# High parts of the weight blocks by a casting DMA from GpSimd in place of a ScalarE cast

## The chip, the cores and the metric

One core of a Trainium2 chip. The metric is the device time of one execution in microseconds, the median of three runs. Engines are called as in the profile: PE (TensorE, with PEld for its weight loads), DVE (VectorE), ACT (ScalarE), POOL (GpSimd), SP (SyncE); SPq is SP's queue of DMA issues.

## The reference

One layer of a streaming encoder on 512 prompt frames and 64 frames of a running stream, model width 1024. All in fp32:

```
proj = rmsnorm(x) @ w_in                      # 1024 x 7880, split by columns
hm   = mlstm(conv(proj_x), proj_v, gates) * sigmoid(proj_o)
ha   = attention(latents of proj_cq, proj_ckv, proj_kr)
p_m  = (hm * silu(proj_z)) @ w_pm
p_a  = (ha * silu(proj_za)) @ w_pa
y    = x + (sigmoid(g_m) * p_m + sigmoid(g_a) * p_a) @ w_out
```

The mLSTM has 4 heads of width 256, the attention 8 heads of 128 + 64. Updated caches and states are outputs too.

## The kernel before

Activations lie transposed, features on the partitions and all T = 576 frames on the free axis. To keep fp32 precision with products in fp32r, every operand is held as a high part (the value rounded to fp32r) and a low part (the rest), and each product is made of three: high x high, high x low and low x high.

A weight block is fetched by `wload` (L103): SP issues the load of `raw` (two buffers), `split_of` (L99) has ACT round it into `whi` and DVE subtract that from `raw` into `wlo` (two buffers each). There are 88 such blocks. 64 of them are blocks of 1024 x 128 weights (56 of w_in, 8 of w_pm, by `fblock`, L146); the others are 8 of w_pa (256 x 512), 4 of w_ukv (256 x 512), 4 of w_uq (384 x 384), 4 of wq_m and wk_m together (two sources of 256 x 256), and 4 of w_out (512 x 256). All are 512 KB but w_uq (576 KB). The blocks of w_ukv and w_uq have their high and low parts in a pool of their own (`cw`), which is opened after the first stage; `wts`, which holds the others, is open from the beginning. The blocks of the first stage (`load_a`, `load_b`) and the second halves of w_out (L843) use `split_of` without `wload`.

A block of `fblock` is multiplied by `gemm_f` (L116) in two halves of 288 frames, each in a PSUM bank of its own (`MM`, L57; one pair of banks, so a half must be emptied before the same half of the next block begins). A half takes whi x high (8 products), whi x low (8), wlo x high (8). The banks are emptied by ACT for the blocks of g_m, g_a, the conv input, the output gate and the values, by DVE also for the two SiLU gates (L520, L685), the added parts of p_a (L597) and p_m (L829).

The order of the work: a first stage (norm, latent projections, mLSTM gates) after START, then attention after PLAN, in which letters stand for tiles of k and q (K), blocks of gates (G, Z), heads (H) and p_a (P); then the mLSTM heads with their blocks between them, p_m, and w_out. The instructions of each engine run in the order of a queue; the framework's scheduler sets that order when the program is built, from its planned times, and inserts the waits. `rsqrt_of` (L74), which every norm uses, is a `pow` on POOL: for k and q tiles (L492, L449: tiles `r`), for the mLSTM chunks (L790: `sc`). POOL issues no DMA.

Of the kernel before, what the change touches and what calls it, by code (L numbers as in the profile page):

```python
# [6 lines left out]
F32 = mybir.dt.float32  # L7
# [3 lines left out]
ALU = mybir.AluOpType  # L11
AX = mybir.AxisListType

P = 128
# [24 lines left out]
def layer(ctx: ExitStack, tc, A, O):  # L39
    nc = tc.nc  # L40
    act, dve, pool, pe, sp = nc.scalar, nc.vector, nc.gpsimd, nc.tensor, nc.sync
# [57 lines left out]
    def split_of(hi, lo, src, eng=None):  # L99
        act.copy(hi, src)  # L100
        (eng or dve).tensor_tensor(lo, src, hi.bitcast(F32), op=ALU.subtract)  # L101

    def wload(srcs, nk, n, wp=None, unit=1024):  # L103
        wp = wp or wts
        shp = lambda t: t[:, 0:nk * n].rearrange("p (k c) -> p k c", k=nk)
        raw = shp(wts.tile([P, 6 * QH], F32, tag="raw", name="raw", bufs=2))
        o = 0
        for s in srcs:
            sp.dma_start(raw[:, o:o + s.shape[0] // P], s.rearrange("(k p) c -> p k c", p=P))
            o += s.shape[0] // P  # L110
        hi = shp(wp.tile([P, unit], F32R, tag="whi", name="whi", bufs=2))
        lo = shp(wp.tile([P, unit], F32R, tag="wlo", name="wlo", bufs=2))
        split_of(hi, lo, raw)
        return hi, lo

    def gemm_f(ps, w, x, nk, c0=0, k0=0):  # L116
# [29 lines left out]
    def fblock(wd, col, x):  # L146
        w = wload([wd[:, col:col + P]], KB, P)
        ps = MM()
        gemm_f(ps, w, x, KB)
        return ps  # L150
# [274 lines left out]
    with ExitStack() as es:  # L425
# [139 lines left out]
        def kq(p):  # L565
            qT = [aq.tile([P, TP], F32, tag="qT", name="qT", bufs=4) for _ in range(2)]
            qrT = aq.tile([P, 2, TP], F32R, tag="qrT", name="qrT", bufs=2)
            for hh in range(2):
                pool.memset(qT[hh][:, T:TP], 0.0)
            pool.memset(qrT.bitcast(F32)[:, :, T:TP], 0.0)  # L570
            kT = [ak.tile([P, TK], F32, tag="kT", name="kT", bufs=4) for _ in range(2)]
            v = ak.tile([P, 6, 2, VD], F32, tag="v", name="v", bufs=2)
            pool.memset(v[DEC:P, 5], 0.0)
            wk = wload([A["w_ukv"][:, 512 * p:512 * (p + 1)]], 2, 512, cw, 6 * QH)
            wq = wload([A["w_uq"][:, 2 * QH * p:2 * QH * (p + 1)]], 3, 2 * QH, cw, 6 * QH)
            run = []
            for g in [k_tile(wk, n, kT, v) for n in range(6)] + [q_tile(wq, n, qT, qrT) for n in range(5)]:
                next(g)
                run.append(g)
                if len(run) > 2:  # L580
                    next(run.pop(0))
            for g in run:
                next(g)
            return qT, qrT, kT, v
# [41 lines left out]
    with ExitStack() as es:  # L626
# [209 lines left out]
        for nb in range(D // NB):  # L836
            cs = slice(nb * NB, (nb + 1) * NB)
            w = [wload([A["w_out"][0:512, cs]], 4, NB)]
            raw = lp.tile([P, 4, NB], F32, tag="gate", name="wraw", bufs=2)
            sp.dma_start(raw, A["w_out"][512:D, cs].rearrange("(k p) c -> p k c", p=P))  # L840
            hi = lp.tile([P, 4, NB], F32R, tag=("qf", "kf")[nb % 2], name="whi2", bufs=1)
            lo = lp.tile([P, 4, NB], F32R, tag=("tm", "ulo")[nb % 2], name="wlo2", bufs=1)
# [69 lines left out]
```

## Time and profile before

| | before |
|---|---|
| median of 3 runs (lowest, highest) | 808.32 us (808.09, 808.92) |
| the profiled execution's own time | 810.22 us |
| its span, first to last instruction | 808.4 us |
| mean granted clock of PE | 0.998 |
| busy PE / DVE / ACT / POOL | 98 / 60 / 45 / 18% |
| data moved by DMA | 72.8 MB |

The profiled execution is one of its own, so sums of its rows are compared with its 810.22 us. Busy time of PE is of pipelined products, whose ends are modelled.

### The profile page before, as it was taken

To read this page: it belongs to the slowest core of one execution; us is meant where nothing else is said; L and a number is where in the kernel's file an instruction comes from. 1 tells how busy PE (TensorE), PEld (TensorE's weight loads), DVE (VectorE), ACT (ScalarE), POOL (GpSimd) and SP (SyncE) were. 2 spreads that over 40 slices of the span, in tenths; PEclk is the share of its full clock that TensorE was granted. 3 is DMA by queue.
4 is the path that set the end of the run, shared out by engine and by line. 5 is a ranking of instruction groups with operands and counts; after the bars stand their busy time and mean duration, and the time that the engine had idled before them with its cause. 6 is when DMAs were issued, how large, how long until landed. Compare 5 with 4: busy or idle time off the path is not lost.

```text
span 808.4 us, 14939 instructions
## 1 busy us (share of the span) xinstructions
PE 791.6 (98%) x5727; PEld 762.3 (94%) x5727; DVE 481.0 (60%) x1240; ACT 362.2 (45%) x991; POOL 148.2 (18%) x286
## 2 busy tenths in 40 slices
PE   7899999999999999989999999999999999999998
PEld 6898998899899898879999999999999999999997
DVE  5567667765686668545535872775587356555421
ACT  5546646663555554414334545444554434322100
POOL 2354331510251134001002111110211111000000
PEclk9999999999999999999999999999999999999999
DMA  8531331023123021314323242333344332533332
GB/s 268 142 110 60 81 108 27 1 54 106 42 53 123 27 67 31 104 35 129 80 79 105 65 119 69 89 85 99 93 129 111 91 87 75 163 111 107 101 102 72
DMA packets 101743, 72.81 MB, mean 90 GB/s; under 512 B 5742, under 2 KB 95848, under 8 KB 101672
## 3 DMA queue, kind: packets, MB, share of 16 engines
q1 hardware_dynamic: 101672, 71.86, 30.8%
q8 instruction: 45, 0.74, 0.4%
q14 instruction: 26, 0.21, 0.1%
HBM read 64.24 MB, written 7.61 MB: 89 GB/s over the span
## 4 chain that ended last, share of the span: by engine, by line
PE 91%; DVE 4%; DMA 3%; ACT 1%; issue 1%; SPq 0%; POOL 0%; ACTq 0%; POOLq 0%
PE mm L122 58%; PE sk L139 9%; PE sa L858 3%; PE sk L858 3%; PE sa L733 2%; PE sa L557 2%; PE sk L733 2%; PE sk L132 2%; PE sa L528 2%; PE sk L750 1%; PE sa L546 1%; PE sa L132 1%; PE sa L530 1%; DMA part<-in_w_in 1%; PE sk L498 1%; DMA E<-gscr 1%
## 5 line engine op out<-in xcount | busy, mean ns | idle before, releaser
L101 DVE TENSOR_TENSOR wlo<-raw,whi 128x1024 fp32r<-128x1024 f32 (+1 forms) x88 | 108.8, 1237 | 95.2 <-ACT whi L100 89.1
L100 ACT CAST whi<-raw 128x1024 fp32r<-128x1024 f32 (+1 forms) x88 | 92.7, 1054 | 136.6 <-PE mm L122 94.1
L122 PE MATMUL mm<-hhi,whi 128*128 128x288 f32 x896 | 146.1, 299 | 1.0 <-ACT hhi L100 1.0
L122 PE MATMUL mm<-hhi,wlo 128*128 128x288 f32 x896 | 146.7, 298 | 0.0
L122 PE MATMUL mm<-hlo,whi 128*128 128x288 f32 x896 | 145.7, 298 | 0.0
L122 PEld LDWEIGHTS mm<-hhi,whi 128*128 128x128 f32 x896 | 126.3, 188 | 2.5 <-ACT hhi L100 1.3
L122 PEld LDWEIGHTS mm<-hlo,whi 128*128 128x128 f32 x896 | 127.1, 188 | 0.9 <-issue 0.5
L122 PEld LDWEIGHTS mm<-hhi,wlo 128*128 128x128 f32 x896 | 127.1, 188 | 0.5
L75 POOL TENSOR_TENSOR r<-r,mhalf 128x2 f32<-128x2 f32 (+3 forms) x44 | 37.0, 841 | 126.1 <-DVE r L491 85.7
L122 PE MATMUL mm<-ha,whi 128*128 128x288 f32 x256 | 50.3, 314 | 2.0 <-ACT ha L100 1.2
L122 PEld LDWEIGHTS mm<-ha,whi 128*128 128x128 f32 x256 | 39.0, 194 | 5.4 <-DVE part L597 2.2
L122 PE MATMUL mm<-ha,wlo 128*128 128x288 f32 x128 | 27.8, 300 | 0.0
L75 POOL TENSOR_TENSOR sc<-sc,mhalf 128x1 f32<-128x1 f32 x20 | 12.1, 605 | 84.9 <-DVE sc L789 84.9
L597 DVE TENSOR_TENSOR part<-part,mm 128x288 f32<-128x288 f32 x48 | 21.2, 449 | 8.6 <-PE mm L122 8.4
L664 POOL MEMSET vf<- 128x64 f32 x8 | 1.2, 152 | 131.8 <-PE sk L673 72.2
L101 POOL TENSOR_TENSOR qi<-qi,qi 128x256 fp32r<-128x256 f32 x16 | 11.8, 737 | 71.6 <-ACT qi L100 71.6
L510 ACT ACTIVATE P<-sa,sc 128x128 f32<-128x128 f32 (+3 forms) x32 | 16.9, 527 | 16.7 <-DVE sc L509 16.5
L528 PE MATMUL sa<-kT,qT 128*128 128x128 f32 (+3 forms) x64 | 22.7, 435 | 0.5 <-ACT qT L470 0.5
L470 ACT ACTIVATE qT<-sk,gqn_c 128x128 f32<-128x128 f32 (+1 forms) x40 | 12.1, 352 | 21.6 <-PE sk L468 21.6
L733 PE MATMUL sk<-va,kw 128*128 128x258 f32 x120 | 21.5, 284 | 0.1
L829 DVE SCALAR_TENSOR_TENSOR mt<-tgm,mm 128x288 f32<-128x288 f32 x16 | 7.3, 454 | 23.9 <-PE mm L122 23.9
L122 PEld LDWEIGHTS mm<-ha,wlo 128*128 128x128 f32 x128 | 21.0, 192 | 0.0
(356 smaller groups left out, 1660.1 us busy)
## 6 DMA issues: line engine op xcount, KB each, us to landing
raw<-in_w_in SPq DMA_DIRECT2D x56, 512.0 KB, 3.9
raw<-in_w_pa SPq DMA_DIRECT2D x8, 512.0 KB
raw<-in_w_pm SPq DMA_DIRECT2D x8, 512.0 KB
raw<-in_w_uq SPq DMA_DIRECT2D x4, 576.0 KB, 4.0
gmscr<-tg SPq DMA_DIRECT2D x8, 288.0 KB
tgm<-gmscr SPq DMA_DIRECT2D x8, 288.0 KB, 2.7
xt<-in_x_prompt SPq DMA_DIRECT2D x4, 512.0 KB, 6.7
raw<-in_w_ukv SPq DMA_DIRECT2D x4, 512.0 KB, 3.4
```

Source lines behind the costliest of these rows:

```text
L75: pool.tensor_tensor(dst, ms, mhalf[0:n, 0:dst.shape[-1]], op=ALU.pow)
L100: act.copy(hi, src)
L101: (eng or dve).tensor_tensor(lo, src, hi.bitcast(F32), op=ALU.subtract)
L122: pe.matmul(ps[j], a[:, k0 + k, c0:c0 + P], b[:, k, sl], start=(n == 0), stop=(n == len(trip) - 1))
L132: pe.matmul(out, x[:, k, t0:t0 + P], a, start=(i == 0), stop=(i == len(trip) - 1))
L139: pe.matmul(out, b[:, k, t0:t0 + L], a[:, k, c0:c0 + n], start=(i == 0), stop=(i == len(trip) - 1))
L510: act.activation(pt[0:L, 0:n], ps, AF.Exp, bias=sc[0:L, 0:1], accum_out=sc[0:L, 1:2])
L528: pe.matmul(ps[:, 0:n], qT[hh][:, q0:q0 + P], kT[hh][:, 0:n], start=True, stop=False)
L557: pe.matmul(of[:, j * P:SEQ], v[:, j, hh], pT[:, off[j]:off[j] + (4 - j) * P], start=(j == 0), stop=(j == 3))
L597: dve.tensor_tensor(part[:, f, sl], part[:, f, sl], ps[j], op=ALU.add)
L733: pe.matmul(out, x, y, start=(first and i == 0), stop=(last and i == 2))
L858: pe.matmul(ps[0:L, 0:NB], x[:, 4 * u + k, t0:t0 + L], w[u][i][:, k], start=(q == 0), stop=(q == len(trip) - 1))
```

## The change

The high part is no longer made by ACT from `raw` but fetched a second time from memory by a DMA that POOL issues and that casts fp32 to fp32r on its way; DVE subtracts it from `raw` as before. A block of two sources takes two such DMAs. The scratch memory for descriptors of DMAs issued by the program is made larger.

```diff
@@ wload @@
         hi = shp(wp.tile([P, unit], F32R, tag="whi", name="whi", bufs=2))
         lo = shp(wp.tile([P, unit], F32R, tag="wlo", name="wlo", bufs=2))
-        split_of(hi, lo, raw)
+        o = 0
+        for s in srcs:
+            pool.dma_start(hi[:, o:o + s.shape[0] // P], s.rearrange("(k p) c -> p k c", p=P))
+            o += s.shape[0] // P
+        dve.tensor_tensor(lo, raw, hi.bitcast(F32), op=ALU.subtract)
         return hi, lo
@@ kernel @@
-    nc = _bacc.Bacc("TRN2", target_bir_lowering=False, num_devices=1, dynamic_dma_scratch_size=1024)
+    nc = _bacc.Bacc("TRN2", target_bir_lowering=False, num_devices=1, dynamic_dma_scratch_size=4096)
```

## Rows read from the trace of the kernel before

**Rows 1.** The page: busy time of each engine, and the granted clock by slices.
```profile
span 808.4 us, 14939 instructions
PE 791.6 (98%) x5727; PEld 762.3 (94%) x5727; DVE 481.0 (60%) x1240; ACT 362.2 (45%) x991; POOL 148.2 (18%) x286
PEclk9999999999999999999999999999999999999999
```

**Rows 2.** Table by stage: length, busy us of each engine, clock, DMA share, GB/s.
```profile
0.00:27.70 27.70, 20.03 (x144) 17.85 (x144) 14.71 (x28) 14.62 (x26) 7.05 (x15) 1.00 0.86 268
...
320.00:366.00 46.00, 43.26 (x277) 38.62 (x277) 24.30 (x64) 13.52 (x33) 0.77 (x5) 0.96 0.26 69
366.00:416.00 50.00, 50.00 (x380) 50.00 (x379) 25.02 (x44) 18.41 (x34) 2.06 (x2) 1.00 0.35 100
...
751.00:808.40 57.40, 53.42 (x450) 53.22 (x449) 17.71 (x32) 5.00 (x6) 1.03 (x2) 1.00 0.29 88
```

**Rows 3.** Groups by line: count, busy us, mean ns, idle time before them and its releasers.
```profile
L101 DVE TENSOR_TENSOR wlo<-raw,whi 128x1024 fp32r<-128x1024 f32 (+1 forms) x88 | 108.8, 1237 | 95.2 <-ACT whi L100 89.1 <-ACT uhi L100 3.9 <-ACT sq L446 1.8
L100 ACT CAST whi<-raw 128x1024 fp32r<-128x1024 f32 (+1 forms) x88 | 92.7, 1054 | 136.6 <-PE mm L122 94.1 <-issue 17.4 <-PE sa L132 8.9
...
L75 POOL TENSOR_TENSOR r<-r,mhalf 128x2 f32<-128x2 f32 (+3 forms) x44 | 37.0, 841 | 126.1 <-DVE r L491 85.7 <-DVE r L448 34.1 <-DVE mrows L379 3.0
...
L757 POOL TENSOR_TENSOR qi<-qf,wi 128x256 f32<-128x256 f32 x16 | 11.8, 735 | 16.3 <-ACT qf L715 15.4
L652 DVE TENSOR_SCALAR acc<-xp,cols 128x579 f32<-128x579 f32 x8 | 4.6, 573 | 0.0
```

**Rows 4.** List of waits: who waited for whom, us in total, times, longest.
```profile
ACT whi L100 <- PE mm L122: 94.1, 52, 8.4
DVE wlo L101 <- ACT whi L100: 89.1, 48, 4.9
...
ACT whi L100 <- DMA raw<-in_w_in: 6.3, 4, 2.8
...
ACT whi L100 <- DMA raw<-in_w_uq: 5.2, 2, 3.1
...
PE mm L122 <- ACT ha L100: 1.2, 1, 1.2
PE mm L122 <- ACT hhi L100: 1.0, 1, 1.0
```

**Rows 5.** Timeline of two plain blocks: start us, us, instruction, idle before.
```profile
376.22 1.05 ACT L100 CAST whi<-raw 128x1024 fp32r<-128x1024 f32 x1 [1.78 <-PE mm L122]
...
377.04 1.22 PE L122 MATMUL mm<-hhi,whi 128*128 128x288 f32 x8
...
383.40 1.21 PE L122 MATMUL mm<-hhi,whi 128*128 128x288 f32 x8
```

**Rows 6.** Source line L109 (ns min/median/max of an issue), and the page's queue.
```profile
L109 SPq DMA_DIRECT2D raw<-in_w_in x56: 367/368/407, 20.6 to 671.0; - x56
...
DMA to landing us min/median/max: 3.4/3.9/4.8
q1 hardware_dynamic: 101672, 71.86, 30.8%
```

**Rows 7.** Timeline of a k tile's norm in the attention.
```profile
213.84 0.69 POOL L75 TENSOR_TENSOR r<-r,mhalf 128x2 f32<-128x2 f32 x1 [1.04 <-DVE r L491]
...
215.05 0.47 DVE L494 TENSOR_SCALAR kn<-kn,r 128x128 f32<-128x128 f32 x2
...
216.10 0.38 PE L498 MATMUL sk<-ident,kn 128*128 128x128 f32 x2
```

**Rows 8.** Timeline of a chunk's norm in an mLSTM head.
```profile
514.02 0.57 POOL L75 TENSOR_TENSOR sc<-sc,mhalf 128x1 f32<-128x1 f32 x1 [2.75 <-DVE sc L789]
...
517.65 0.38 PE L794 MATMUL sa<-ident,hn 128*128 128x128 f32 x2
```

**Rows 9.** Timeline of the first stage: POOL's first work, the first block's load.
```profile
0.34 0.10 POOL L888 MEMSET const-uint8-127<- 128x1 uint8 x1
6.40 0.55 POOL L75 TENSOR_TENSOR st<-st,mhalf 128x1 f32<-128x1 f32 x1 [5.96 <-DVE st L256]
...
20.59 0.40 SPq L109 DMA_DIRECT2D raw<-in_w_in  x1
```

## The prediction

> **What bounds the kernel now.** I read the page's busy shares first. TensorE (PE) is busy 791.6 of 808.4 us and the granted clock stands at full speed almost everywhere, while DVE, ACT and POOL are busy 481, 362 and 148 us [rows 1]. The table by stage shows where PE's missing 16.8 us lie [rows 2]: 7.7 us in the first 27.7 us, which is a stage of loads (DMA share 0.86), 4.0 us in the last stage (the stores of the result), and only 808.4 - 791.6 - 7.7 - 4.0 = 5.1 us in everything between. In the stretches of plain blocks PE has no gap at all. So whatever an engine beside PE saves, no more than some 5 us can come back, unless the two ends get shorter.
>
> The groups by line then give the work at stake [rows 3]: 88 casts `whi<-raw` on ACT (92.7 us) and 88 subtractions `wlo<-raw,whi` on DVE (108.8 us). The list of waits says how they stand in their queues [rows 4]. ACT sits 94.1 us, 52 times, until PE lets go of the old `whi`, and DVE 89.1 us, 48 times, until ACT's cast is done: 1.86 us each, and PE loses nothing by it. These casts are made as soon as the buffer is free, and much earlier than they are needed. The timeline of two plain blocks shows how much earlier [rows 5]: the cast starts at 376.22, when PE releases the buffer, and the block that reads it begins at 383.40. That is 7.18 us. Blocks begin at 377.04 and 383.40, so a block of 48 products lasts 6.36 us, or 0.1325 us a product; lo is first read 16 products into a block, 2.1 us later.
>
> **What goes.** 88 ACT casts, 92.7 us of an engine that is 45% busy. ACT does not bound any stage, so the cast is worth what of the 5.1 us it releases: 0 to 5.1 us. Most of those gaps lie at 320 to 366 us (2.74 us), in the stretch of the output projection of the attention. I take half, 2.7 us.
>
> **What comes: the copy by DMA.** 92 transfers on POOL's queue (88 blocks, the q/k block of each of 4 heads from two sources). 64 of them (w_in and w_pm) are cut into 1024 rows of 512 B, the others into 256 to 512 longer rows. The trace has no DMA of POOL's. Two prices are missing.
>
> (a) What POOL spends on issuing one: X. From below: SP issues the same pattern in 0.37 us [rows 6]. From above: GpSimd works through 256 columns in 735 ns [rows 3], 2.87 ns a step; four steps for each of 1024 rows would be 11.8 us. I take one step per row, 2.9 us: the elementwise row is of the engine that has to issue, SP's is of another.
>
> (b) The transfer. The same 512 KB land 3.9 us after SP's issue began [rows 6], 3.5 us without the issue. The twin transfer and the cast can make it longer; from below 3.5, from above see the fourth rival. I take 3.5.
>
> So hi is ready X + 3.5 = 6.4 us after the release, where ACT took 1.05 us. In a stretch of plain blocks 7.18 us are at hand, so PE reads it in time, with 0.8 us left. Cover is gone at X = 3.7 us; beyond it each of the 64 long blocks stalls by the excess.
>
> The Trainium skill ("SBUF — State Buffer", section "SBUF: two separate sides") warns that descriptors of a GpSimd-issued DMA can't be written while DVE runs an operation in a 2-port mode, such as an fp32 copy within SBUF. Such a one-input DVE operation of the conv takes 0.57 us [rows 3]; by that rule a transfer that meets one would be left with 0.2 us of the 0.8, and the second rival would begin at X = 3.1 instead of 3.7 us. The trace of before has no DMA from GpSimd and can't say.
>
> (c) DVE's queue. The subtraction now waits for a landing. The order of DVE's instructions is fixed from planned times, and landings came later than planned where one was close: ACT waited 6.3 us in 4 cases for w_in and 5.2 us in 2 for w_uq [rows 4], 1.9 us each. If each of the 48 waits of DVE grows from 1.86 by 1.9 to 3.76 us, what is queued behind it matters: PE's two PSUM banks of a block are emptied half by half, so an evacuation has half a block, 3.2 us, before PE stalls. The excess is 3.76 - 3.2 = 0.56 us a time. Only blocks whose banks DVE reads suffer: the 8 + 8 SiLU gates, the p_m blocks and the added parts of p_a; the others (8 each of g_m, g_a, conv, o, v) are emptied by ACT, which waits for nothing now. So I count half of the 48: 24 x 0.56 = 13.4 us. From below 0 (the planner puts the subtraction later); from above the whole delay 6.4 - 1.05 = 5.35 us at all 48, 48 x (1.86 + 5.35 - 3.2) = 192 us.
>
> (d) POOL's queue. Behind an issue stand the `pow` operations of the norms. In the attention a `pow` ends at 214.53, its DVE scaling starts at 215.05, and PE reads that at 216.10 with 0.6 us to spare [rows 7]. Between 60 and 366 us 15 blocks of 1024 rows (2.9 us) and 16 of 256 to 384 rows (0.7 to 1.1 us) make some 57 us of issuing, 19% of the stretch. Of the 44 `pow`s of k and q tiles 19% would meet one and wait 1.45 us on the mean, 0.85 us over the slack: 7 us. POOL has idle time ahead of these (126 us in all [rows 3]), into which the planner can put issues; I take half, 3.5 us. In the mLSTM heads 3 us lie between the `pow`'s end and PE's use [rows 8], so nothing is lost there. From below 0; from above, at X = 11.8, each of the 15 long issues costs PE all but the slack, 15 x 11.2 = 168 us.
>
> (e) The start. The first two blocks' `whi` buffers are free from the beginning and POOL is idle from 0.4 to 6.4 us [rows 9], while SP issues the first block's raw load only at 20.59, behind the loads of the first stage. If POOL issues its two at once, 1.05 MB go ahead of them; at the first stage's 268 GB/s that is 3.9 us. If the planner holds them back, 0. I take half, 2 us.
>
> (f) Traffic. The 88 blocks are 46.4 MB again on top of 71.86 MB, at 30.8% of 16 engines [rows 6]: 30.8 x 118.3/71.9 = 51%. In the plain-block stretch, at share 0.35 for 100 GB/s, a block in 6.36 us adds 82 GB/s and 0.29: 0.64. Hidden, at a plain copy's rate. The larger scratch costs no time itself.
>
> **Sum.** +13.4 + 3.5 + 2 - 2.7 = +16.2 us. The profiled execution took 810.2 us (span 808.4 and 1.8 us around it), so 826 us of its own; the median of the runs is 808.3, and so I say 808.3 + 16.2, rounded **825 us**. A change under 0.2% (1.6 us) is about what a measurement of this kernel can't tell from none.
>
> **Rivals.**
> First: issuing is cheap (X under 1 us), planned well, and the landing is hidden. Then (c) and (d) vanish; with (e) and the gain near each other the time is 807 to 810 us, the same. For it: DVE's waits of 1.86 us cost nothing today. Against it: landings came 1.9 us later than planned. The Trainium skill ("DMA: Bandwidth & Descriptors", section "Anatomy of one DMA — SWDGE (gpsimd) path") speaks for it: it says many descriptors can be emitted before that shows, and gives 2.0 us + bytes/436e3, an estimate of 3.2 us for a block; by that page alone the sum would be this rival's. The landing of 3.9 us from SP [rows 6] is of that size. Chance 0.14.
>
> Second: X is above the cover of 3.7 us. At X = 4.6 us each of 64 blocks stalls 0.9 us: +58 us over the loss of the forecast's kind, some 870 to 890 us; at 6.4 us and more POOL can't keep up with one block per 6.36 us. Chance 0.12.
>
> Third, the other side: ACT's release is worth the whole 5.1 us and neither queue loses. ACT's casts stood among PSUM evacuations, and PE's small waits for ACT (`ha`, `hhi`, 1.0 to 1.2 us each [rows 4]) go away. 808.3 - 5.1 = 803 us. It decides when the landing is at least 1 us earlier than DVE's turn and no first transfer is moved ahead of the start. Against it: PE's gaps are few and not mainly ACT's. Chance 0.18.
>
> Fourth: the casting transfer is slow. At c times a plain copy's engine time the plain-block stretch is full at 0.35 + 0.29c = 1, c = 2.2; at c = 4 a block takes 1.5 x 6.36 = 9.6 us, 64 x 3.2 = +205 us, over 1000 us. Nothing in the trace speaks for or against. Chance 0.09.
>
> That leaves 0.47 for the forecast. Its own range is 810 us ((d) alone, less the gain: 808.3 + 0.8) to 850 us (the excess at all 48 waits, 27, with all of (d) and (e), 7 + 3.9, and no gain: 846). Faster 0.18, same 0.14, slower 0.68. Range: 803 (the third rival's time) to 880 (half of the second rival's lies within); what is left out, the fourth, half of the second and a little below, is some 0.16.
>
> **What would show it.** In the profile of the changed kernel: ACT busy down by 93 us to some 270; packets doubled for the weights and a DMA share near 51%; DVE's wait at `wlo` now for a DMA and over 3 us each (c); `pow`s that start late after a POOL issue (d); PE's first product after the 27.7 us of before (e). A POOL issue of under 1 us, or DVE's waits unchanged at 2 us, would make me wrong towards the first and third rivals; issues over 4 us or a DMA share near 0.9 in the plain blocks towards the other two.

## The result, and the profile after

The changed kernel takes 854.9 us (median of four runs, 854.3 to 856.0), the kernel before 808.6 us beside it: a ratio of 1.0566 [1.0551, 1.0581], 46.3 us slower where 16.7 were forecast. The sign is right and the time lies in the range of 803 to 880 us; the loss is 2.8 times the one forecast. The tables below are each of one profiled execution, whose spans differ by some us between executions of the same kernel, so differences of a us or two between them mean little.

The page of the changed kernel: busy time, clock by slices, the two DMA queues (q0 carries POOL's copies, q1 SP's loads and stores), the group of the subtraction (now L117).

```profile
span 852.5 us, 15031 instructions
...
PE 807.9 (95%) x5727; PEld 770.1 (90%) x5727; DVE 485.0 (57%) x1240; ACT 274.2 (32%) x903; POOL 233.1 (27%) x378
...
PEclk7999999999999999998999999999999999999999
...
q0 software_dynamic: 75712, 46.41, 30.0%
q1 hardware_dynamic: 101672, 71.86, 29.7%
...
L117 DVE TENSOR_TENSOR wlo<-raw,whi 128x1024 fp32r<-128x1024 f32 (+1 forms) x88 | 109.6, 1246 | 145.3 <-DMA whi<-in_w_in 53.7
```

ACT works 88.0 us less, DVE about as long as before, and POOL 84.9 us more, which is mostly the issues; none of the three is near to being full [rows 1]. PE does the same 5727 instructions, 16.3 us longer, and stands still for 852.5 - 807.9 = 44.6 us instead of 16.8. So 27.8 us of the 44.1 us of span are new gaps, and 16.3 us are the same products taking longer; the mean granted clock, 0.984 against 0.998 before, makes some 0.014 x 807.9 = 11.3 of these, an estimate.

To see where, I cut both traces at the same events of the program: the store of the first latents, the end of the products with `ha`, the first and last product of the mLSTM heads' key blocks (`uhi`), the first and last product of p_m (`hmhi`). The table by stage of the changed kernel (length, busy us of PE, PEld, DVE, ACT, POOL, clock, DMA share, GB/s):

```profile
0.00:46.60 46.60, 39.02 (x236) 36.27 (x237) 23.82 (x46) 20.67 (x42) 12.79 (x22) 0.85 0.73 201
46.60:386.10 339.50, 323.18 (x2069) 292.03 (x2068) 213.54 (x655) 139.44 (x567) 113.80 (x208) 0.99 0.44 108
386.10:456.70 70.60, 60.84 (x443) 59.94 (x442) 28.48 (x55) 11.54 (x29) 11.83 (x19) 0.95 0.75 153
456.70:681.30 224.60, 221.13 (x1702) 219.61 (x1701) 139.29 (x340) 77.46 (x208) 61.50 (x86) 1.00 0.74 159
681.30:739.40 58.10, 58.10 (x455) 58.05 (x453) 32.66 (x75) 15.94 (x43) 15.44 (x20) 1.00 0.69 150
739.40:792.90 53.50, 50.07 (x370) 48.90 (x369) 29.15 (x41) 6.36 (x11) 14.48 (x22) 1.00 0.84 200
...
```

The lengths of the same seven stages in all profiled executions, in us:

| kernel | start | attention | turn | heads | blocks after | p_m | rest | span |
|---|---|---|---|---|---|---|---|---|
| before | 40.9 | 323.0 | 58.3 | 219.8 | 58.1 | 48.8 | 59.5 | 808.4 |
| after | 46.6 | 339.5 | 70.6 | 224.6 | 58.1 | 53.5 | 59.6 | 852.5 |
| e1 first two by ACT | 41.0 | 343.0 | 70.7 | 226.6 | 58.0 | 52.9 | 59.7 | 851.9 |
| e2 four buffers | 49.9 | 325.0 | 58.4 | 220.2 | 58.1 | 48.8 | 59.6 | 820.0 |
| e3 lo without hi | 45.3 | 323.2 | 60.5 | 220.2 | 58.1 | 50.2 | 59.7 | 817.2 |
| e4 copy not used | 48.5 | 398.0 | 58.4 | 219.7 | 58.1 | 48.8 | 59.6 | 891.1 |
| e5 the same, two buffers | 53.7 | 375.4 | 58.4 | 219.8 | 58.1 | 48.8 | 59.6 | 873.8 |
| e6 only lo by the copy | 45.2 | 330.3 | 58.4 | 223.8 | 58.1 | 48.7 | 59.7 | 824.2 |
| e7 four buffers, start by ACT | 40.8 | 329.2 | 58.3 | 220.0 | 58.2 | 48.7 | 59.7 | 814.9 |
| e8 before, four buffers | 40.7 | 324.4 | 59.4 | 230.2 | 58.2 | 48.7 | 59.5 | 821.1 |
| e9 copy paced | 48.3 | 325.7 | 59.2 | 235.5 | 58.1 | 48.8 | 58.8 | 834.4 |
| e10 three buffers, start by ACT | 40.6 | 328.1 | 59.0 | 219.7 | 58.1 | 48.7 | 59.7 | 813.9 |
| e11 copies after the attention | 41.1 | 322.7 | 67.5 | 226.8 | 58.1 | 52.5 | 59.7 | 828.4 |
| e12 copies up to there | 45.6 | 337.5 | 58.4 | 219.7 | 58.0 | 48.8 | 59.6 | 827.6 |

The loss sits in five places: start 5.7, attention 16.5, the turn from attention to heads 12.3, heads 4.8, p_m 4.7. The plain blocks after the heads lose nothing, with as much traffic (share 0.69). The clock is below full in the start and at the turn (0.85 and 0.95). In the start PE's gaps sum to 7.6 us, as before (7.7): what is longer there is the products, 39.0 us for 33.2.

The source line of the copies (L115, ns min/median/max of an issue), who waited for them (us, times) and their landings:

```profile
L115 POOL DMA_DIRECT2D whi<-in_w_in x56: 876/937/1026, 1.3 to 724.2; - x56
L115 POOL DMA_DIRECT2D whi<-in_w_pa x8: 698/726/906, 123.3 to 360.1; - x8
...
  DVE wlo L117: 102.0, 55
...
DMA to landing us min/median/max: 3.0/4.7/16.4
```

The list of waits of the changed kernel (us in all, times, longest):

```profile
POOL whi L115 <- PE mm L126: 210.4, 49, 17.9
DVE wlo L117 <- DMA whi<-in_w_in: 53.7, 32, 6.0
...
DVE wlo L117 <- DMA whi<-in_w_pm: 15.9, 6, 3.9
...
DVE E L728 <- DMA E<-gscr: 15.1, 4, 4.4
...
PE mm L126 <- DMA whi<-in_w_in: 6.7, 1, 6.7
...
DVE qs L456 <- POOL r L75: 6.0, 7, 1.2
...
PE sk L502 <- DVE kn L498: 4.0, 4, 2.8
...
PE mm L126 <- DVE mt L833: 3.4, 5, 1.5
DVE kn L498 <- POOL r L75: 3.3, 5, 0.9
...
PE mm L126 <- DVE tz L689: 2.3, 2, 1.7
...
PE mm L126 <- DVE part L601: 2.0, 3, 1.4
...
PE sa L541 <- DVE qrT L475: 1.9, 1, 1.9
```

Three things are to be seen. POOL holds the copy back until PE lets go of the old `whi`, 49 times: the copy starts as late as ACT's cast did [rows 4]. DVE then waits for copies at `wlo`, with all sources 102.0 us in 55 times, or 1.85 us each, no longer than the 1.86 of before. And PE has no wait for `wlo` at all; it waits for DVE's other work: `kn` (the normalised k), `qrT` (the rotary part of q, transposed), and the banks that DVE empties (`mt` in p_m, `tz` in the gates, `part` in p_a).

How that comes about is in the timeline of the attention (start us, us, instruction, idle before):

```profile
274.96 0.99 POOL L115 DMA_DIRECT2D whi<-in_w_in  x1 [5.18 <-PE mm L126]
...
278.38 0.72 POOL L75 TENSOR_TENSOR r<-r,mhalf 128x2 f32<-128x2 f32 x1 [2.43 <-DVE r L495]
...
280.95 1.22 DVE L117 TENSOR_TENSOR wlo<-raw,whi 128x1024 fp32r<-128x1024 f32 x1 [2.40 <-DMA whi<-in_w_in]
...
282.16 0.48 DVE L498 TENSOR_SCALAR kn<-kn,r 128x128 f32<-128x128 f32 x2
...
282.50 0.33 PE L502 MATMUL sk<-ident,kn 128*128 128x128 f32 x1 [2.75 <-DVE kn L498]
...
294.81 1.21 PE L126 MATMUL mm<-hhi,whi 128*128 128x288 f32 x8
```

The buffer is free at 274.96, the copy is there at 280.95, 6.0 us later, and DVE stands for 2.40 us with the scaling of k behind it, whose factor POOL had ready at 279.10. PE stands for 2.75 us until `kn` is there. The next block of w_in begins only at 294.81: the subtraction was in no hurry, `kn` was. Ten of PE's waits of over 0.4 us for DVE, 12.3 us together, are of this kind: six in the attention, four in p_m, each behind a wait of the subtraction for a landing, with DVE at work from there on.

In p_m the order of DVE's queue is another one too. Two blocks, the first of the kernel before, the second of the change:

```profile
725.83 0.46 DVE L829 SCALAR_TENSOR_TENSOR mt<-tgm,mm 128x288 f32<-128x288 f32 x1 [2.04 <-PE mm L122]
...
726.20 1.22 DVE L101 TENSOR_TENSOR wlo<-raw,whi 128x1024 fp32r<-128x1024 f32 x1
```
```profile
772.77 1.23 DVE L117 TENSOR_TENSOR wlo<-raw,whi 128x1024 fp32r<-128x1024 f32 x1 [2.63 <-DMA whi<-in_w_pm]
...
773.91 0.81 DVE L833 SCALAR_TENSOR_TENSOR mt<-tgm,mm 128x288 f32<-128x288 f32 x2
...
774.42 1.33 PE L126 MATMUL mm<-hmhi,whi 128*128 128x288 f32 x8 [0.70 <-DVE mt L833]
```

Before, the subtraction stood behind the `mt` that empties a block's second bank; for the change the scheduler has put it ahead of both. Of the kernels in the table only after, e1 and e11 have that order, and they are the three in which p_m is 3.7 to 4.7 us longer; in the others it is at most 1.4.

At the turn the copy itself is late (timeline of all engines, below it PE's own, then the table by stretch for PE: length, busy, clock, DMA share, GB/s):

```profile
384.94 0.45 SPq L701 DMA_DIRECT2D hgB<-in_hnorm_g  x1
...
385.44 0.42 SPq L725 DMA_DIRECT2D E<-gscr  x1
...
385.91 0.53 SPq L726 DMA_DIRECT2D wi<-gscr  x1
...
386.48 1.03 SPq L748 DMA_DIRECT2D Cf<-in_state_C  x1
...
386.82 0.88 POOL L115 DMA_DIRECT2D whi<-in_w_in  x1 [7.24 <-PE mm L126]
...
399.58 1.23 DVE L117 TENSOR_TENSOR wlo<-raw,whi 128x1024 fp32r<-128x1024 f32 x1 [5.97 <-DMA whi<-in_w_in]
```
```profile
391.81 1.23 PE L126 MATMUL mm<-hhi,wlo 128*128 128x288 f32 x8
399.70 2.26 PE L126 MATMUL mm<-hhi,whi 128*128 128x288 f32 x8 [6.66 <-DMA whi<-in_w_in]
```
```profile
385.00:393.10 8.10, 8.03 (x60) 1.00 0.61 160
...
399.70:401.75 2.05, 2.05 (x8) 0.50 0.08 9
```

It comes 12.7 us after its issue, behind four loads of the heads that SP had issued in the 1.9 us before. PE stands for 6.66 us, and its next eight products take 2.26 us instead of 1.23: the granted clock, 1.00 ahead of the gap, is 0.50 behind it, the lower of its two levels (1.2 GHz for 2.4).

### The profile page after: what moved, and what is told of

Read it like the earlier page. It is cut to its first block, busy times and chain, and to the rows that moved or that the text cites. A ratio compares the mean times of both kernels' runs of the same rounds, so it can differ in the third digit from the quotient of the medians.

```text
span 852.5 us, 15031 instructions
## 1 busy us (share of the span) xinstructions
PE 807.9 (95%) x5727; PEld 770.1 (90%) x5727; DVE 485.0 (57%) x1240; ACT 274.2 (32%) x903; POOL 233.1 (27%) x378
## 3 DMA queue, kind: packets, MB, share of 16 engines
q0 software_dynamic: 75712, 46.41, 30.0%
q1 hardware_dynamic: 101672, 71.86, 29.7%
## 4 chain that ended last, share of the span: by engine, by line
PE 59%; DMA 20%; issue 8%; DVE 8%; POOL 2%; ACT 2%; SPq 0%; POOLq 0%; DVEq 0%; ACTq 0%
PE mm L126 38%; DMA whi<-in_w_in 8%; PE sk L143 5%; PE sk L862 3%; PE sa L862 3%; DMA whi<-in_w_pa 3%; DMA E<-gscr 2%; DMA whi<-in_w_pm 2%; DVE wlo L117 2%; PE sa L737 2%; DMA rif<-in_w_in 1%; PE sk L737 1%; PE sa L532 1%; PE sa L136 1%; PE sa L561 1%
## 5 line engine op out<-in xcount | busy, mean ns | idle before, releaser
L117 DVE TENSOR_TENSOR wlo<-raw,whi 128x1024 fp32r<-128x1024 f32 (+1 forms) x88 | 109.6, 1246 | 145.3 <-DMA whi<-in_w_in 53.7
L126 PE MATMUL mm<-hhi,whi 128*128 128x288 f32 x896 | 147.6, 302 | 12.3 <-DMA whi<-in_w_in 6.7
L126 PE MATMUL mm<-hhi,wlo 128*128 128x288 f32 x896 | 150.0, 300 | 0.0
L126 PEld LDWEIGHTS mm<-hhi,whi 128*128 128x128 f32 x896 | 128.1, 190 | 15.1 <-issue 6.9
L115 POOL DMA_DIRECT2D whi<-in_w_in x56 | 52.0, 928 | 165.5 <-PE mm L126 152.8
L101 POOL TENSOR_TENSOR qi<-qi,qi 128x256 fp32r<-128x256 f32 x16 | 13.6, 852 | 45.0 <-ACT qi L100 45.0
L126 PE MATMUL mm<-hmhi,whi 128*128 128x288 f32 x128 | 20.2, 300 | 3.4 <-DVE mt L833 3.4
L532 PE MATMUL sa<-kT,qT 128*128 128x128 f32 (+3 forms) x64 | 22.7, 436 | 0.0
L126 PEld LDWEIGHTS mm<-hmhi,whi 128*128 128x128 f32 x128 | 17.7, 189 | 4.6 <-DVE mt L833 4.6
L100 ACT CAST hhi<-mt 128x576 fp32r<-128x576 f32 x8 | 5.4, 673 | 50.3 <-DVE mt L834 50.3
L504 ACT ACTIVATE kT<-sk,cols 128x128 f32<-128x128 f32 (+1 forms) x48 | 14.8, 356 | 19.4 <-PE sk L502 19.3
```

The source lines that it names most:

```text
L115: pool.dma_start(hi[:, o:o + s.shape[0] // P], s.rearrange("(k p) c -> p k c", p=P))
L117: dve.tensor_tensor(lo, raw, hi.bitcast(F32), op=ALU.subtract)
L126: pe.matmul(ps[j], a[:, k0 + k, c0:c0 + P], b[:, k, sl], start=(n == 0), stop=(n == len(trip) - 1))
L504: act.activation(kT[hh][:, t0:t0 + L], ps2[:, hh * P:hh * P + L], AF.Copy, scale=gkn_c)
L532: pe.matmul(ps[:, 0:n], qT[hh][:, q0:q0 + P], kT[hh][:, 0:n], start=True, stop=False)
```

## The experiments

All are edits of `wload` of the changed kernel, but e8. The scheduler plans anew for each, and the order of DVE's queue differs from the change's in every one of them: what an experiment shows is the edit together with its order, and no run has one without the other. The kernel before ran beside them at 809.26 us (e1 to e4), 808.79 (e5 to e8) and 808.85 (e9 to e12). The theory that I held after the result: copies come later after the release of the buffer than ACT's cast did, and DVE's queue carries that to PE. The rivals: the second stream of traffic delays other loads, or POOL's issues delay POOL's `pow`s.

**e1, the first two blocks by ACT** (are the two copies at 1.27 us the loss of the start?)

```diff
+    blocks = []
...
+        blocks.append(wp is wts)
+        if wp is wts and sum(blocks) <= 2:
+            split_of(hi, lo, raw)
+            return hi, lo
```

> The changed kernel, but the first two blocks (the ones whose copies were issued at 1.3 us, ahead of the first stage's loads) have their high part cast by ACT again. If those 1.05 MB are what moved the first stage by 5.7 us (first store of the latents 40.94 to 46.60 us): about 849 us. If the first stage is late for another reason (a new order of the queues): 854 to 856.

850.4 us, 1.0504 [1.0467, 1.0542]. The start is back at 41.0 us, so the two copies were its whole loss. By the medians 4.6 us of it stay gained (5.2 against the kernel before beside each); in the profiled execution (853.7 us, the slowest of the four) the attention took 3.5 us more than after's. The other losses stand.

**e2, four buffers for the high parts**: the copy can be issued two blocks earlier; its length, the traffic and POOL's issues stay.

```diff
-        hi = shp(wp.tile([P, unit], F32R, tag="whi", name="whi", bufs=2))
+        hi = shp(wp.tile([P, unit], F32R, tag="whi", name="whi", bufs=4 if wp is wts else 2))
```

> The changed kernel with four buffers for the high parts of the plain blocks instead of two, so that a copy can be issued two blocks earlier. If the loss after the first stage (44 - 5.7 = 38 us) is lateness, a copy that may start only when PE lets go of a buffer and lands 4.9 us later where ACT took 1.05: most of it returns, 815 to 825 us. If it is traffic or POOL's share of the work: 845 to 855.

821.4 us, 1.0153 [1.0114, 1.0191]. The table by stage of e2 from the attention to the heads, then one of its waits:

```profile
49.90:374.90 325.00, 318.29 (x2065) 290.81 (x2064) 214.50 (x655) 141.00 (x567) 115.40 (x208) 0.99 0.47 115
374.90:433.30 58.40, 58.40 (x445) 58.40 (x443) 28.67 (x55) 11.65 (x29) 11.85 (x19) 1.00 0.87 180
433.30:653.50 220.20, 219.89 (x1703) 219.42 (x1701) 138.91 (x340) 76.22 (x208) 61.34 (x86) 1.00 0.74 163
```
```profile
DVE wlo L117 <- PE mm L126: 69.3, 34, 4.1
```

Of the 38.4 us that were lost behind the start 2.6 are left. The median landing is still 4.7 us, the DMA share is as high as after's or higher (0.47, 0.87, 0.74), and POOL spends the same time; what has moved is the moment of the issue, and with it the order of DVE's queue (in p_m it is that of before). DVE's waits of 2 us at `wlo` are still there, but now they end with PE's release of the old `wlo` and cost next to nothing. PE has no wait for `kn` or `mt` any more. The start is worse by 9.0 us: four copies go ahead of the first loads.

**e3, the subtraction without the high part** (`raw - raw`, so the low parts are zero): all copies as in the change, read by PE, but DVE doesn't wait for them.

```diff
-        dve.tensor_tensor(lo, raw, hi.bitcast(F32), op=ALU.subtract)
+        dve.tensor_tensor(lo, raw, raw, op=ALU.subtract)
```

> The changed kernel, but the subtraction reads raw twice and not the high part (the low parts are zero), so DVE waits for no copy while PE still does. If what stands behind DVE's blocked subtraction makes the loss: 820 to 830 us. If PE (or POOL's queue) waits for the copies itself: 845 us or more.

819.7 us, 1.0122 [1.0096, 1.0149]. Behind the start 8.8 - 4.4 = 4.4 us of the 38.4 are left. So DVE's dependence on the copy, with the order that the scheduler chose for it, is worth 34.0 us; PE's own is small. PE's waits for `kn` and `mt` are gone here too.

**e4 and e5, the copy made but not used** (a `twin` tile, read by nobody; ACT casts as before; e4 one buffer, e5 two): traffic and issues, with no wait of DVE or PE for a copy. The edit of e4 (e5 has its `twin` in `wts`, for all blocks):

```diff
+        twin = shp(wp.tile([P, unit], F32R, tag="twin", name="twin", bufs=1))
...
-            pool.dma_start(hi[:, o:o + s.shape[0] // P], s.rearrange("(k p) c -> p k c", p=P))
+            pool.dma_start(twin[:, o:o + s.shape[0] // P], s.rearrange("(k p) c -> p k c", p=P))
...
-        dve.tensor_tensor(lo, raw, hi.bitcast(F32), op=ALU.subtract)
+        split_of(hi, lo, raw)
```

> ACT casts the high part as before, and POOL issues the casting copy of every block too, into a tile of its own that nobody reads. All of the traffic and all of POOL's issues, no wait for a copy on PE or DVE. If lateness makes the loss: the 5.7 us of the first stage and little more, 813 to 820 us. If traffic makes it: 840 to 855 us.

> As the run with the unused copy, but with two buffers for the copies, so that POOL no longer stands behind the landing of the copy just issued. There 83 us were lost before the end of the attention, with DVE waiting 80 us for POOL's pows, and none after it. If POOL's blocked queue made that loss: 813 to 820 us, the first stage's 5.7 us and a little of the rest. If traffic in the attention made it: 850 us or more again.

e4 894.2 us, 1.1046 [1.1012, 1.1080]; e5 877.1 us, 1.0844 [1.0824, 1.0864]. e4 lies above what either theory said, e5 where traffic was to put it (850 us or more). They tell little about the change: nothing paces these copies but their own landing, so they run far ahead (the DMA share in the attention is 0.78 and 0.84, where the change has 0.44), and POOL stands behind the one under way while its `pow`s wait. How much of their loss is traffic was not separated. Waits of e4:

```profile
POOL twin L116 <- DMA twin<-in_w_in: 139.1, 48, 5.9
...
DVE kn L499 <- POOL r L75: 45.9, 21, 11.6
...
DVE qs L457 <- POOL r L75: 34.6, 16, 6.6
```

In e5 the last copy is issued at 274.3 us, so its later stages, as long as those of before, had no second stream in them. What e4 shows is what an issue costs that waits at the head of POOL's queue: DVE waits 80.5 us for `pow`s in e4, against 9.3 in the changed kernel.

**e6, only the low part by the copy** (`twin`, two buffers, feeds the subtraction; ACT casts `whi` for PE): DVE's wait alone.

```diff
...
+        act.copy(hi, raw)
+        dve.tensor_tensor(lo, raw, twin.bitcast(F32), op=ALU.subtract)
```

> ACT casts the high part that PE reads, as before; POOL copies into a tile of its own (two buffers), and DVE subtracts that copy, so that DVE alone waits for the copies and PE never does. It is the counterpart of the run in which PE waited and DVE didn't (817 us of span). If the blocked queue of DVE carries the loss: 840 to 855 us. If PE's own wait does: 813 to 820.

826.0 us, 1.0215 [1.0198, 1.0232]. Between the theories, and not the test that it was meant to be: here DVE's subtraction frees the buffer, so the copies start earlier than in the change, and DVE waits only 12.8 us, 7 times, for one. Still 11.5 us are lost behind the start (attention 7.3, heads 4.0), which that wait doesn't account for; in the heads PE waits 3.4 us for `kw` (the weighted k), which stands behind DVE's wait for the load of `E` (the decay matrix of a head, 13.3 us in e6).

**e7, e2 with the first four blocks by ACT**, and **e10, three buffers with the first three by ACT**.

> Four buffers for the high parts, and the first four plain blocks, whose copies would be issued ahead of the first stage's loads, cast by ACT. The run with four buffers lost 9 us in the first stage and 2 us after it, so: 808 to 812 us. If the start's gain is given back later, as with two buffers: 815 to 822.

> Three buffers for the high parts, the first three plain blocks by ACT: one block of lead more than the changed kernel, one fewer than the run of 815.5 us with four. A block is 6.4 us and a copy lands 4.7 us after its issue, so if lateness is the loss one block is enough: 812 to 818 us. If the loss falls step by step with the buffers: 825 to 835.

e7 815.5 us, 1.0081 [1.0066, 1.0096]; e10 814.5 us, 1.0065 [1.0047, 1.0083]. One buffer more and an undisturbed start take back 40 of the 46 us. The rest lies in the attention (e10 5.1 us, e7 6.2, so that e7 came out in the second of its two ranges). In e10 the largest waits of PE there that before doesn't have are 1.3 us for `ckhi` and 1.9 for `tg`, both of ACT; what delays them is open. e10 is the best version here, and it does not beat the kernel before.

**e8, the kernel before with four buffers for the high parts**, a control: is it the buffers that help?

> The kernel before with four buffers for the high parts and nothing else changed, a control: ACT's casts are early enough there, so within 2 us of 808.6. If four buffers alone make this kernel faster, 800 to 805, part of what they gave the changed kernel was not lateness.

822.4 us, 1.0165 [1.0150, 1.0180]; slower, where no change was expected. Waits of e8:

```profile
ACT whi L100 <- DMA raw<-in_w_in: 108.5, 56, 13.0
```

With a buffer free, ACT's cast stands at the head of ACT's queue until `raw` lands, and what is behind it waits, for PE most of all `kf` (the k of a head), 5.2 us: the changed kernel's fault on another engine. The heads lose 10.4 us. More buffers don't help by themselves; they help a copy that doesn't wait for `raw`.

**e9, the copy not used, but paced** (the next copy behind an addition on POOL that reads the last `twin` and ACT's `whi`): traffic at about the change's times.

```diff
...
+        for t, h in prev:
+            pool.tensor_tensor(sink, t, h.bitcast(F32)[:, 0, 0:1], op=ALU.add)
...
+        prev.append((twin.bitcast(F32)[:, 0, 0:1], hi))
```

> ACT casts the high part for PE and DVE as before, POOL copies each block into a tile nobody computes with, and a one-column addition on POOL that reads the block's high part and its copy holds the next copy back until this block is cast, so that the copies run along with the blocks over the whole kernel (in the two runs with unused copies they had run ahead and were over by the attention's end). Traffic, issues and a blocked queue of POOL's, no wait of PE's or DVE's. If lateness makes the loss: 812 to 820 us, most of it at the start. If traffic and POOL's queue make it: 835 to 855.

836.0 us, 1.0336 [1.0315, 1.0357], just inside the range of traffic and POOL's queue, not that of lateness. By stages it is not one or the other: the start loses 7.4 us; the attention loses 2.7 us of the change's 16.5 and the turn 0.9 of 12.3, at shares of 0.49 and 0.96. The heads lose 15.7. Waits of e9:

```profile
ACT E L737 <- DVE E L736: 20.2, 4, 6.5
DVE E L736 <- DMA E<-gscr: 18.6, 4, 5.9
...
PE mm L134 <- ACT to L692: 10.1, 3, 3.6
```

There the load of `E`, once a head, comes late, DVE and ACT stand for it, and PE for what is behind it on ACT, `to` (the output gate). The change has nearly as long a wait for `E` (15.1 us), and PE waits 1.0 us for `to`: again what stands behind a wait sets its price.

**e11, copies only after the attention**, and **e12, only up to there** (ACT's cast in the other part).

> The first stage and the attention with ACT's casts, the copies only in the blocks after it. If the losses of the stages are their own: the attention's 16.5 and the start's 5.7 us return and the turn's 12.3, the heads' 4.8 and p_m's 4.9 stay: 828 to 832 us. If the turn's loss was brought over from the attention: 815 to 822.

> The counterpart: the copies in the first stage and the attention, ACT's casts after it. If the stages' losses are their own: 808.6 + 22 = 829 to 833 us, the two together giving the changed kernel's 46 us.

e11 831.8 us, 1.0291 [1.0250, 1.0333]; e12 831.6 us, 1.0289 [1.0266, 1.0312]. 23.0 and 22.7 us, 45.7 together, of the change's 46.3: each part loses its own, and neither causes the other's, as far as e11's runs let one say (829.9 to 837.6 us).

## Why the prediction was right in sign and too small

**The step that failed** is the size of (c): "an evacuation has half a block, 3.2 us, before PE stalls. The excess is 3.76 - 3.2 = 0.56 us a time", for half of 48 waits, 13.4 us. The mechanism is the one that happened, DVE's queue behind a landing; the size was 34.0 us (e3 against after, behind the start, the new order included).

Two things made it larger. The cover was less than 3.2 us: an evacuation behind the subtraction waits for the subtraction's own 1.23 us too. In four blocks of p_m waits of 2.63 to 3.86 us with 1.23 behind them are 0.7 to 1.9 us more than 3.2, an estimate, and PE lost 0.4 to 1.5 each time. And the sum counted evacuations alone: in the attention `kn`, `qrT` and the softmax stand behind the subtraction, with no half block of slack. The lower bound of (c) had the planner put the subtraction later; in p_m it put it earlier.

The waits did not grow to 3.76 us: they stayed at 1.85. With issues under 1 us and waits of 2 us, both signs that were to point to the first and third rivals appeared, and the time went the other way. A wait's length on DVE says little of its price. e2 has waits of 69.3 us there that cost next to nothing, for they end at the moment when PE lets go of a buffer. In the change they end at such a moment plus issue and landing (6.0 us in the timeline above, 1.05 us with ACT's cast [rows 5]); in that time PE goes on and comes to need DVE's other work. That timeline and the nine waits like it show this step. That DVE's wait for a late copy makes the loss is shown by e3, which takes the wait away, and by e2, which moves the issue. How much of it is the lateness itself, and how much the place in the queue that the scheduler gave the subtraction because of it, is open: no run has the late copy in the old order.

That the time lies in the stated range is partly luck: it is above the forecast's own 810 to 850 us, where the range reached for the second rival, whose condition (an issue of over 3.7 us) did not hold.

**(a) The issue**: forecast 2.9 us, measured 0.94 (0.73 for the 256-row blocks). The first of rival one's conditions held, but the landing was not hidden, and its time didn't follow. By the Trainium skill's page "DMA: Bandwidth & Descriptors", section "Anatomy of one DMA — SWDGE (gpsimd) path", many descriptors can be emitted before that shows; four times the rows for 0.2 us more agrees. The estimate of 3.2 us for a block by its formula doesn't: 4.7 us at the median. The Trainium skill's port rule ("SBUF — State Buffer", section "SBUF: two separate sides"), by which the second rival would have begun earlier, did not show: no issue took over 1.03 us, and the 25 copies issued while DVE ran a one-input operation on SBUF tiles landed after 4.7 us at the median, like the others.

**(b) The landing**: high part ready 6.4 us after the release, of that 3.5 of transfer. Measured 4.7 us with the issue at the median, within the 7.18 us that were at hand, and PE waits for `whi` only once, at the turn. Right for PE, where it was used; its tail, 12.7 us at the turn, was not forecast.

**(d) POOL's queue**: 3.5 us forecast, nothing found. DVE's waits for the `pow`s of k and q are 9.3 us (`qs` 6.0, `kn` 3.3), where they were 13.5 us before (6.7 and 6.8). e4 shows what it would have been with landings in that queue.

**(e) The start**: two copies ahead of the first loads, as described, at 1.27 us. Forecast 2, measured 5.7; e1 gives it back. The bound of 3.9 counted the bytes at 268 GB/s; at the casting stream's 1.56 times per byte (below) it would be 6.1, an estimate. The copies land only 11 to 16 us after their issue, and PE runs the stage at a clock of 0.85 where it had 1.00; but e3 and e12, with the same two copies and clocks of 0.96 and 0.93, still lose 4.4 and 4.7 us, so the clock is not most of it.

**(f) Traffic**: share forecast 51%, measured 30.0 + 29.7%. The casting stream takes as much engine time for 46.41 MB as the plain one for 71.86, 1.56 times per byte, c = 1.56 in the fourth rival's terms, short of its 2.2 (both streams mix rows of several lengths). "Hidden" is right where loads are early: e2 runs the turn at 0.87 and the heads at 0.74 within 0.4 us of before. It is not right in general: DVE waits for `E` 18.6 us in e9 and 15.1 us in the change, where it was 7.2 before. But in e2, e3 and e10, with the same traffic in the heads, it waits 7.0 to 7.9 us and the heads lose at most 0.4, so traffic alone doesn't make `E` late. At the turn the copy is late behind SP's loads; an earlier issue cures it (e2), and without DVE's wait 2.2 us of the 12.3 are left (e3). How much is queueing and how much the late issue was not separated.

**The gain** of 2.7 us for ACT's release was not seen: e10, with the least loss, is in no stage more than 0.3 us shorter than before. Inside the attention, where e10 loses 5.1 us, it could be hidden.

**Not in the sum** was the clock: some 11 us of longer products by the estimate above, half of them in the start, where most of the loss comes without it too (e3, e12). At the turn the stall cost more than its own length: 6.66 us, and 1.03 more for the next eight products.

## What to carry to other kernels

Before an operation is moved to a path of longer latency, count the time from the release of its buffer to its result, not its throughput. If that grows, it needs a buffer more (three instead of two, with an undisturbed start, took back 40 of 46 us here), or its reader must not stand ahead of urgent work in an in-order queue: price a late operand by what is queued behind its reader, not by the length of the reader's wait. A scheduler may change that order with the edit, so compare the queues before and after. And a queue that waits for nothing issues at time zero, ahead of the loads that the start needs; give the first blocks to another path.

## What the runs showed of the hardware

A casting DMA from POOL costs 0.94 us of POOL for 1024 rows of 512 B, 0.73 for 256, and 1.56 times the DMA engines' time per byte of the plain stream beside it (1.4 in e12, 1.8 in e6; rows of several lengths in both). It lands after 4.7 us at the median, 11 to 16 us in the start, where the DMA share is 0.73. An issue that waits blocks POOL's computations behind it (e4: 80.5 us of DVE waiting for `pow`s). After a gap of 6.66 us PE's granted clock was 0.50 in the next 2.05 us, and in the start 0.85 on the mean where it had been 1.00, with gaps that sum to 7.6 us and 7.7.
